# Gate and up projections with seven block products instead of eight, the middle channels in two rounds

## The chip, the cores and the metric

The kernel runs on one core of a Trainium2 chip. The metric is device time in microseconds (us) of one execution. TensorE is PE in the rows, VectorE DVE, ScalarE ACT, GpSimd POOL, and SyncE's queue, which issues the loads, SP.

## The reference

Two layers over 512 tokens of 1024 channels. Each layer has two feed-forward (FFN) parts around a mixer, and a per-layer embedding step at its end:

```python
def swiglu(x, w_gate, w_up, w_down):
    return (jax.nn.silu(x @ w_gate) * (x @ w_up)) @ w_down
...
for l in range(DEPTH):
    h = h + 0.5 * swiglu(rms_norm(h, ffn1_norm[l]), ffn1_w_gate[l], ffn1_w_up[l], ffn1_w_down[l])
    h = h + hybrid_mixer(rms_norm(h, mix_norm[l]), ...)
    h = h + 0.5 * swiglu(rms_norm(h, ffn2_norm[l]), ffn2_w_gate[l], ffn2_w_up[l], ffn2_w_down[l])
    gate = jax.nn.sigmoid(rms_norm(h, ple_norm[l]) @ ple_w_gate[l])
    h = h + gate * (p[l] @ ple_w_proj[l])
return rms_norm(h, final_norm)
```

The middle width of the FFN is 2816, that is 22 tiles of 128 channels; all data are float32.

## The kernel before

Channels lie on the partitions, the 512 tokens along the rows, so the residual stream `hT` is 8 tiles of 128x512. A float32 product is made of three products of float32r parts: each operand is split into a high and a low part (ACT copies the high part, DVE subtracts it from the value), and `mm3` issues high x high, high x low and low x high into one PSUM bank. Weights come in raw tiles `wr` of 512 KB (three buffers, loaded from SP) and are split into `wh` and `wl` (two buffers each).

PE takes its matmuls in the order in which they are written down. The other engines run their instructions in an order that the scheduler fixed when the program was built; each engine runs its own list strictly from front to back, so an instruction that waits holds all that stand behind it.

An FFN loops over the 22 middle tiles. For each it makes the gate product `pg` and the up product `pu`, 8 channel tiles x 3 matmuls of 128x512 each, and then `gated` works on the pair on DVE and ACT. The norm of the row isn't in the operand: the row factor `rb` is worked out beside the first products (`norm.sums` and `norm.rows`, which PE issues at the two places that `at` names) and multiplied in after the product. Then 8 output tiles `pd` of 22 x 3 matmuls follow, and after each one `residual` work on DVE and the split of the next part's operand (`Norm.add`).

There are four FFN parts: the first at the start of the program, the second behind the mixer's output projection (`pwo`), the third behind the embedding step of layer 0 (`ppg`), the fourth behind the second mixer.

## Time and profile before

| | |
|---|---|
| median of 3 runs | 2087.9 us (2087.01 to 2090.97) |
| profiled execution: span from first to last instruction | 2086.9 us (the profile gives no other time of this execution) |
| PE busy | 2042.6 us, 98% |
| DVE busy | 1108.8 us, 53% |
| ACT busy | 740.0 us, 35% |

The busy time of PE counts every matmul with its drain, and these overlap, so two neighbours are better compared by their starts. Whether PE really waits shows where its busy time in a window is below the window's length.

### The profile page before, as it was taken

What the parts mean: (1) busy time and instruction counts of PE and PEld (TensorE: products, weight loads), DVE (VectorE), ACT (ScalarE), POOL (GpSimd) and SP (SyncE); (2) the same over time, 40 slices, a digit from 0 to 9 for tenths busy, and PEclk for the clock granted to TensorE, in tenths of its full rate; (3) what the DMA queues carried; (4) which work ended last, traced back from release to release, by engine and by line L of the source; (5) the groups of instructions that cost most, each with busy time, mean ns of one, the idle gap of its engine ahead of it and who ended that gap; (6) DMA issues with size and microseconds to landing.
All of it is one profiled execution on the core that took longest, in us unless ns stands there. A gap on an engine that the chain in (4) does not pass through costs nothing.

```text
span 2086.9 us, 24214 instructions
## 1 busy us (share of the span) xinstructions
PE 2042.6 (98%) x9529; PEld 1666.5 (80%) x9529; DVE 1108.8 (53%) x1958; ACT 740.0 (35%) x1188; POOL 189.7 (9%) x166
## 2 busy tenths in 40 slices
PE   9999999998999999999999999999899999999997
PEld 6888888877778888888878888888676888888886
DVE  5444433779855444433754444337997644443346
ACT  4232223355643232223532222224475432222233
POOL 1000001052110000000100000000521100000002
PEclk9999999999999999999999999999999999999998
DMA  5323233311032223333323233333110332333331
GB/s 185 101 91 101 89 92 102 97 51 54 9 101 91 98 94 98 90 97 109 101 92 101 92 100 89 98 96 99 56 34 21 105 98 92 100 93 95 98 99 61
DMA packets 56290, 186.35 MB, mean 89 GB/s; under 512 B 6384, under 2 KB 9712, under 8 KB 55920
## 3 DMA queue, kind: packets, MB, share of 16 engines
q1 hardware_dynamic: 56176, 184.81, 28.3%
q8 instruction: 74, 1.21, 0.2%
q14 instruction: 40, 0.33, 0.0%
HBM read 182.69 MB, written 2.10 MB: 89 GB/s over the span
## 4 chain that ended last, share of the span: by engine, by line
PE 90%; DVE 6%; ACT 2%; issue 1%; DMA 1%; POOL 0%; SPq 0%; DVEq 0%; ACTq 0%; POOLq 0%
PE pd L141 8%; PE pd L143 8%; PE pu L143 8%; PE pd L142 8%; PE pu L142 8%; PE pu L141 8%; PE pg L143 8%; PE pg L142 7%; PE pg L141 7%; PE pp L141 2%; PE pp L143 2%; PE pp L142 2%; PE pwo L143 1%; PE pwo L141 1%; PE pwo L142 1%; PE ppg L142 1%
## 5 line engine op out<-in xcount | busy, mean ns | idle before, releaser
L117 ACT ACTIVATE wh<-wr 128x1024 fp32r<-128x1024 f32 (+1 forms) x346 | 356.9, 1031 | 1140.5 <-issue 741.7
L118 DVE TENSOR_TENSOR wl<-wr,wh 128x1024 fp32r<-128x1024 f32 (+1 forms) x334 | 397.8, 1191 | 355.8 <-ACT wh L117 355.6
L222 POOL TENSOR_TENSOR acc<-acc,sq 128x512 f32<-128x512 f32 (+1 forms) x55 | 80.8, 1469 | 1589.9 <-ACT sq L221 1589.3
L282 DVE TENSOR_TENSOR gs<-th,pu 128x512 f32<-128x512 f32 x88 | 60.4, 688 | 219.9 <-PE pu L143 219.9
L141 PE MATMUL pd<-h,wh 128*128 128x512 f32 x448 | 175.1, 391 | 0.0
L278 DVE TENSOR_TENSOR gs<-pg,rb 128x512 f32<-128x512 f32 x88 | 60.5, 691 | 215.6 <-PE pg L143 215.6
L143 PE MATMUL pd<-h,wl 128*128 128x512 f32 x448 | 174.8, 390 | 0.0
L142 PE MATMUL pd<-l,wh 128*128 128x512 f32 x448 | 174.3, 389 | 0.0
L141 PE MATMUL pg<-B,wh 128*128 128x512 f32 x352 | 138.0, 392 | 2.4 <-ACT wh L122 1.6
L143 PE MATMUL pu<-A,wl 128*128 128x512 f32 x352 | 138.7, 394 | 0.0
L143 PE MATMUL pg<-A,wl 128*128 128x512 f32 x352 | 138.7, 394 | 0.0
L143 PE MATMUL pg<-B,wl 128*128 128x512 f32 x352 | 138.4, 393 | 0.1
L142 PE MATMUL pg<-B,wh 128*128 128x512 f32 x352 | 137.8, 392 | 0.6 <-DVE B L212 0.6
L143 PE MATMUL pu<-B,wl 128*128 128x512 f32 x352 | 138.3, 393 | 0.0
L142 PE MATMUL pg<-A,wh 128*128 128x512 f32 x352 | 137.9, 392 | 0.0
L142 PE MATMUL pu<-A,wh 128*128 128x512 f32 x352 | 137.9, 392 | 0.0
L141 PE MATMUL pu<-B,wh 128*128 128x512 f32 x352 | 137.7, 391 | 0.0
L142 PE MATMUL pu<-B,wh 128*128 128x512 f32 x352 | 137.3, 390 | 0.0
L141 PE MATMUL pg<-A,wh 128*128 128x512 f32 x352 | 136.9, 389 | 0.0
L141 PE MATMUL pu<-A,wh 128*128 128x512 f32 x352 | 136.7, 388 | 0.0
L143 PE MATMUL pp<-B,wl 128*128 128x512 f32 x240 | 97.3, 405 | 6.6 <-DVE wl L118 6.6
L141 PE MATMUL pp<-B,wh 128*128 128x512 f32 x240 | 99.8, 416 | 0.0
(354 smaller groups left out, 3921.3 us busy)
## 6 DMA issues: line engine op xcount, KB each, us to landing
wr<-in_g_dram SPq DMA_DIRECT2D x87, 512.0 KB, 3.5
wr<-in_u_dram SPq DMA_DIRECT2D x87, 512.0 KB, 3.4
wr<-in_d_dram SPq DMA_DIRECT2D x64, 512.0 KB, 3.6
wr<-in_wi_dram SPq DMA_DIRECT2D x30, 512.0 KB, 3.4
wr<-in_d_dram SPq DMA_DIRECT2D x32, 384.0 KB, 3.1
wr<-in_pg_dram SPq DMA_DIRECT2D x16, 512.0 KB, 3.4
wr<-in_wo_dram SPq DMA_DIRECT2D x8, 512.0 KB, 3.5
wr<-in_wt_dram SPq DMA_DIRECT2D x8, 392.0 KB, 3.0
```

The costliest lines, as they stand in the source:

```text
L117: A.activation(out=hi, in_=raw, func=AF.Copy)
L118: (via or V).tensor_tensor(out=lo, in0=raw, in1=hi.bitcast(F32), op=ALU.subtract)
L141: T.matmul(out=out, lhsT=wh, rhs=xh, start=start, stop=False)
L142: T.matmul(out=out, lhsT=wh, rhs=xl, start=False, stop=False)
L143: T.matmul(out=out, lhsT=wl, rhs=xh, start=False, stop=stop)
L222: (V if k == KD - 1 else G).tensor_tensor(out=acc, in0=acc, in1=sq, op=ALU.add)
L278: V.tensor_tensor(out=gs, in0=pg, in1=norm.rb, op=ALU.mult)
L282: V.tensor_tensor(out=gs, in0=th, in1=pu, op=ALU.mult)
```

## The change

Two middle tiles, two halves of the 1024 channels (4 tiles each) and two halves of the tokens (256 each) make a product of 2x2 blocks. The change forms each such product by Strassen's scheme (in Winograd's form): 7 block products in place of 8. What was 2 x 8 x 3 matmuls of 512 columns becomes 7 x 4 x 3 matmuls of 256 columns. Such a block product for gate or for up is called a unit here; an FFN has 22 units (11 for the gate, 11 for up, in turn), the program 88.

- The operand side needs sums of blocks. `Norm.upper` and `Norm.lower` form them where the split of the operand stood, for each pair of channel tiles q and q + 4, and split each sum into two parts.
- The weight side needs four sums. `load` reads the 16 blocks' rows of a unit by three loads from SP (512, 512 and 256 KB) and one more 512 KB read that POOL issues and that adds into the second tile (`r2`, two buffers). `combine` forms the other sums with two DVE additions (L408 and L409 of the changed kernel) and splits the results. The names are A12 and A11 (split from the raw tile `r1`), S4 (split into `sh`, `sl`), S3 and S1 (from `r2`), A22 and S2 (from `r3`).
- `Unit.p` issues a block product (12 matmuls) and the copies and sums of its results: L463 and L464 after product 1, L467 after 7, L470 after 6, L472 after 4, L474 after 5. PE's order in a unit is 2, 1, 3, 7, then 5 of the unit before, then 6 and 4. In the first two units of an FFN it is 2 and 3 of both units (three of the four channel pairs, then the fourth), and then the rest.
- The middle channels go in two rounds (5 and 6 pairs of tiles); the down projection runs after each, with the residual added twice.
- The mixer's work buffers go from 20 to 14, and other tiles of it share the operand's places.

The rest of the diff renames tiles and moves loads. In the diff, `groups` are buffers for 8 blocks of split weights: five, used in turn.

```diff
-AT0 = (23, 31)
-AT1 = (15, 23)
-# columns of the constants
+AT0 = (12, 15)
+AT1 = (8, 12)
+NP = NF // 2
+ROUNDS = ((0, 5), (5, 11))
+NX = 4
...
+    class Combined:
+        def __init__(self):
+            self.t = {}
+        def at(self, part, n):
+            i = NT28 // 2 * part + n
+            if i not in self.t:
+                self.t[i] = place(i)
+            return self.t[i]
+        def __call__(self, part, name, q):
+            if name == "B11":
+                return self.at(part, 12 + q // 2)[:, H * (q % 2):H * (q % 2) + H]
+            n, c = {"B22": (0, 0), "B21": (0, H), "T3": (1, 0), "t2": (1, H), "t1": (2, 0), "T4": (2, H)}[name]
+            return self.at(part, 3 * q + n)[:, c:c + H]
...
+        def gained(self, k, cs, hi, lo):
             h, gk = hT[:, k, cs], self.gain[:, k:k + 1]
-            A.activation(out=self.xh[k][:, cs], in_=h, func=AF.Copy, scale=gk)
-            V.scalar_tensor_tensor(out=self.xl[k][:, cs], in0=h, scalar=gk, in1=self.xh[k][:, cs].bitcast(F32),
+            A.activation(out=hi, in_=h, func=AF.Copy, scale=gk)
+            V.scalar_tensor_tensor(out=lo, in0=h, scalar=gk, in1=hi.bitcast(F32), op0=ALU.mult, op1=ALU.subtract)
+        def split(self, k, t512, cs=ALL):
+            if not self.x:
+                self.gained(k, cs, self.xh[k][:, cs], self.xl[k][:, cs])
+            elif k < 4:
+                if cs.stop == S:
+                    self.upper(k, t512)
+            else:
+                self.lower(k - 4, cs)
+        def upper(self, q, t512):
+            x, h, gk = self.x, hT[:, q, :], self.gain[:, q:q + 1]
+            g, t14, t32 = t512("tg"), t512("t14"), t512("t32")
+            self.raw[q] = g, t14, t32
+            self.gained(q, HALVES[1], x(0, "B11", q), x(1, "B11", q))
+            A.activation(out=g[:, 0:H], in_=h[:, 0:H], func=AF.Copy, scale=gk)
+            V.scalar_tensor_tensor(out=t14[:, 0:H], in0=h[:, H:S], scalar=gk, in1=g[:, 0:H],
                                    op0=ALU.mult, op1=ALU.subtract)
+            split(t14[:, 0:H], x(0, "t1", q), x(1, "t1", q))
+        def lower(self, q, cs):
+            x, h = self.x, hT[:, q + 4, :]
+            gk, nk = self.gain[:, q + 4:q + 5], self.neg[:, q + 4:q + 5]
+            g, t14, t32 = self.raw[q]
+            self.gained(q + 4, cs, x.both(0, 0, q)[:, cs], x.both(1, 0, q)[:, cs])
+            if cs.start == 0:
+                V.scalar_tensor_tensor(out=t32[:, 0:H], in0=h[:, 0:H], scalar=gk, in1=g[:, 0:H],
+                                       op0=ALU.mult, op1=ALU.subtract)
+                V.scalar_tensor_tensor(out=t32[:, H:S], in0=h[:, 0:H], scalar=nk, in1=t14[:, 0:H],
+                                       op0=ALU.mult, op1=ALU.subtract)
+                split(t32, x.both(0, 1, q), x.both(1, 1, q))
+            if cs.stop == S:
+                V.scalar_tensor_tensor(out=t14[:, H:S], in0=h[:, H:S], scalar=nk, in1=t32[:, H:S],
+                                       op0=ALU.mult, op1=ALU.subtract)
+                split(t14[:, H:S], x(0, "T4", q), x(1, "T4", q))
...
+            groups = iter(range(1 << 20))
+            def group(k, n):
+                i = next(groups) % 5
+                if i < 2:
+                    return [whp.tile([128, k, n], F32R, tag=t, name=t) for t in ("wh", "wl")]
+                return [fp.tile([128, k, n], F32R, tag=t, name=t, bufs=3) for t in ("gh", "gl")]
+            def halfgroup():
+                return [fp.tile([128, 4, 128], F32R, tag=t, name=t, bufs=2) for t in ("sh", "sl")]
...
+            def load(j, m):
+                src = a[f"{m}{which}"][l, j]
+                r1 = loaded(src[:, 0:8], 8)
+                r2 = fp.tile([128, 8, 128], F32, tag="r2", name="r2", bufs=2)
+                nc.sync.dma_start(out=r2, in_=src[:, 4:12])
+                G.dma_start(out=r2.rearrange("p k n -> p (k n)"), in_=src[:, 8:16].rearrange("p k n -> p (k n)"),
+                            accum_op=ALU.add)
+                r3 = wrp.tile([128, 8, 128], F32, tag="wr", name="wr")
+                nc.sync.dma_start(out=r3[:, 0:4], in_=src[:, 12:16])
+                return r1, r2, r3
+            def combine(r1, r2, r3):
+                w = {}
+                def put(raw, *names):
+                    g = group(8, 128) if len(names) == 2 else halfgroup()
+                    split(raw, *g)
+                    for i, n in enumerate(names):
+                        w[n] = [t[:, 4 * i:4 * i + 4] for t in g]
+                put(r1, "A12", "A11")
+                V.tensor_tensor(out=r3[:, 4:8], in0=r2[:, 4:8], in1=r1[:, 4:8], op=ALU.add)
+                V.tensor_tensor(out=r1[:, 0:4], in0=r1[:, 0:4], in1=r3[:, 4:8], op=ALU.add)
+                put(r1[:, 0:4], "S4")
+                put(r2, "S3", "S1")
+                put(r3, "A22", "S2")
+                return w
+            def product(ps, w, wn, xn, start, stop, qs=range(4)):
+                (wh, wl), more = w[wn], not (start and stop)
+                for q in qs:
+                    xh, xl = x(0, xn, q), x(1, xn, q)
+                    for i, (l_, r_) in enumerate(((wh, xh), (wh, xl), (wl, xh))):
+                        T.matmul(out=ps, lhsT=l_[:, q, :], rhs=r_, start=start and q == 0 and i == 0,
+                                 stop=stop and q == 3 and i == 2, skip_group_check=more)
+            count = iter(range(1 << 20))
...
+            def gated(cg, cu, hi, lo):
+                rb = norm.rb.unsqueeze(1).to_broadcast([128, 2, S])
+                V.tensor_tensor(out=cg, in0=cg, in1=rb, op=ALU.mult)
+                th = ft.tile([128, 2, S], F32, tag="th", name="th")
+                for i in range(2):
+                    A.activation(out=th[:, i, :], in_=cg[:, i, :], func=AF.Tanh, scale=0.5 - i)
+                V.scalar_tensor_tensor(out=th, in0=th, scalar=1.0, in1=cg, op0=ALU.add, op1=ALU.mult)
+                V.tensor_tensor(out=th, in0=th, in1=cu, op=ALU.mult)
+                split(th, hi, lo)
...
+                def p(self, n, qs=range(4)):
+                    ps, wn, xn, start, stop = {
+                        1: (self.X[:, 1], "A11", "B11", True, False), 2: (self.X[:, 0], "A12", "B21", True, True),
+                        3: (self.Y[:, 0], "S4", "B22", True, True), 7: (self.Y[:, 1], "S3", "T3", True, False),
+                        6: (self.X[:, 1], "S2", "t2", False, False), 4: (self.Y[:, 1], "A22", "T4", False, True),
+                        5: (self.X[:, 1], "S1", "t1", False, True)}[n]
+                    product(ps, self.w, wn, xn, start, stop, qs)
+                    if 3 not in qs:
+                        return
+                    with tc.high_priority():
+                        if n == 1:
+                            self.c = ft.tile([128, 2, S], F32, tag="c" + self.m, name="c" + self.m)
+                            c11 = self.c[:, 0, H:S]
+                            A.activation(out=c11, in_=self.X[:, 0], func=AF.Copy)
+                            V.tensor_tensor(out=c11, in0=c11, in1=self.X[:, 1], op=ALU.add)
+                        if n == 7:
+                            self.ys = ft.tile([128, 2, H], F32, tag="ys", name="ys", bufs=2)
+                            A.activation(out=self.ys, in_=self.Y, func=AF.Copy)
+                        if n == 6:
+                            self.e = ft.tile([128, H], F32, tag="e", name="e", bufs=2)
+                            A.activation(out=self.e, in_=self.X[:, 1], func=AF.Copy)
+                        if n == 4:
+                            V.tensor_tensor(out=self.c[:, 1, H:S], in0=self.e, in1=self.Y[:, 1], op=ALU.add)
+                        if n == 5:
+                            V.tensor_tensor(out=self.c[:, :, 0:H], in0=self.X[:, 1].unsqueeze(1).to_broadcast([128, 2, H]),
+                                            in1=self.ys, op=ALU.add)
+                    taken()
...
+            src = a[f"d{which}"]
+            for r, (j0, j1) in enumerate(ROUNDS):
+                last = None
+                us = list(range(2 * j0, 2 * j1))
+                if r == 0:
+                    prepare(0)
+                    prepare(1)
+                    pair = [begin(u, r) for u in (0, 1)]
+                    for qs in (range(3), range(3, 4)):
+                        for unit in pair:
+                            unit.p(2, qs)
+                            unit.p(3, qs)
+                    gate, up = pair
+                    prepare(2)
+                    for n in (1, 7, 6, 4):
+                        gate.p(n)
+                    up.p(1)
+                    gate.p(5)
+                    for n in (7, 6, 4):
+                        up.p(n)
+                    last = up
+                    us = us[2:]
+                for u in us:
+                    unit = begin(u, r)
+                    if u + 1 < 2 * j1:
+                        prepare(u + 1)
+                    for n in (2, 1, 3, 7):
+                        unit.p(n)
+                    close(last)
+                    for n in (6, 4):
+                        unit.p(n)
+                    if unit.m == "g":
+                        gate = unit
+                    last = unit
+                close(last)
...
+                    pds = {}
+                    for d in range(KD):
+                        pds[d] = bank([128, S], "pd")
+                        down(pds[d], grouped(loaded(src[l, d][:, 0:8, :], 8), 8), range(8), range(8), True, False)
+                        if d == 0:
+                            continue
+                        for e in ((0, 1) if d == 1 else (d,)):
+                            end(e)
+                        if d == KD - 2:
+                            prepare(2 * j1)
...
-            dp = es.enter_context(tc.tile_pool(name="dp", bufs=20))
-            lp = es.enter_context(tc.tile_pool(name="lp", bufs=1))
-            ap_ = es.enter_context(tc.tile_pool(name="ap", bufs=1))
+            tp = es.enter_context(tc.tile_pool(name="tp", bufs=1, reuse_waits="tile"))
+            lp = es.enter_context(tc.tile_pool(name="lp", bufs=1, reuse_waits="tile"))
+            ap_ = es.enter_context(tc.tile_pool(name="ap", bufs=1, reuse_waits="tile"))
+            dp = es.enter_context(tc.tile_pool(name="dp", bufs=14, reuse_waits="tile"))
...
-            o[f"{n}{w}"] = i[f"ffn{w}_w_{s}"].reshape(L, KD, 128, NF, 128).transpose(0, 3, 2, 1, 4)
+            b = i[f"ffn{w}_w_{s}"].reshape(L, 2, 4, 128, NP, 2, 128)
+            b = np.stack([b[:, c, :, :, :, r] for r, c in ((0, 1), (0, 0), (1, 0), (1, 1))], 4)
+            o[f"{n}{w}"] = b.transpose(0, 3, 2, 4, 1, 5).reshape(L, NP, 128, 16, 128)
```

The order of instructions on DVE, in the steady part of an FFN. Before, the products of a pair of middle tiles are followed by the splits of the next weights (`wl`) and by the gating (L278, L281, L282, L123); `pg` and `pu` are the products:

```order
L278 TENSOR_TENSOR gs_5430<-pg_5374,rb_4969 128x512
L118 TENSOR_TENSOR wl_5441<-wr_5438,wh_5440 128x1024
L281 SCALAR_TENSOR_TENSOR th_5432<-th_5432,gs_5430 128x512
L282 TENSOR_TENSOR gs_5430<-th_5432,pu_5405 128x512
L118 TENSOR_TENSOR wl_5472<-wr_5469,wh_5471 128x1024
L123 TENSOR_TENSOR B15_4843<-gs_5430,B7_4835 128x512
```

After the change, in the second round of the first FFN. `cg_2672<-e_2736,qg_2622` (L472) is the last result of the unit that ends; it waits for the last product of that unit. `wr_2623` is the raw tile `r1` of the unit that PE takes next, `sh`/`sl` are the parts of its S4, `wr_2753`, `wr_2758` and `r2_2755` are the tiles of the unit after that, and X4/X5 are the parts of a gated result:

```order
L129 TENSOR_TENSOR gl_2631<-wr_2623,gh_2630 128x1024
L472 TENSOR_TENSOR cg_2672<-e_2736,qg_2622 128x256
L129 TENSOR_TENSOR X5_2715<-th_2717,X4_2714 128x1024
L409 TENSOR_TENSOR wr_2623<-wr_2623,wr_2628 128x512
L129 TENSOR_TENSOR gl_2761<-wr_2753,gh_2760 128x1024
L408 TENSOR_TENSOR wr_2758<-r2_2755,wr_2753 128x512
L129 TENSOR_TENSOR sl_2637<-wr_2623,sh_2636 128x512
```

The split of S4 for a unit stands behind L472 of the unit before and four more instructions.

The order on DVE where the second FFN starts. Before: `pwo_4778` is the last tile of the output projection, A14 and A15 are low parts of the operand, L222 is the last sum of squares:

```order
L997 TENSOR_TENSOR hT_75<-hT_75,pwo_4778 128x512
L118 TENSOR_TENSOR wl_4880<-wr_4877,wh_4879 128x1024
L212 SCALAR_TENSOR_TENSOR A15_4621<-hT_75,par_73,A7_4613 128x512
L222 TENSOR_TENSOR acc_4475<-acc_4475,sq_4806 128x512
L118 TENSOR_TENSOR wl_4938<-wr_4935,wh_4937 128x1024
L237 TENSOR_SCALAR nv_4913<-ssc_4908 128x4
```

After the change (the last additions to `hT` and its blocks stand just ahead): T25 is an operand part of the last channel pair, `wr_6163`, `wr_6168` and `r2_6165` belong to the first gate unit, `wr_6188`, `wr_6193` and `r2_6190` to the first up unit:

```order
L243 TENSOR_SCALAR neg_9857<-par_73 128x8
L129 TENSOR_TENSOR T25_6095<-t14_6088,T11_6094 128x256
L408 TENSOR_TENSOR wr_6168<-r2_6165,wr_6163 128x512
L409 TENSOR_TENSOR wr_6163<-wr_6163,wr_6168 128x512
L129 TENSOR_TENSOR wl_6181<-r2_6165,wh_6180 128x1024
L129 TENSOR_TENSOR gl_6185<-wr_6168,gh_6184 128x1024
L129 TENSOR_TENSOR gl_6196<-wr_6188,gh_6195 128x1024
L408 TENSOR_TENSOR wr_6193<-r2_6190,wr_6188 128x512
L129 TENSOR_TENSOR gl_6206<-r2_6190,gh_6205 128x1024
L129 TENSOR_TENSOR sl_6177<-wr_6163,sh_6176 128x512
L409 TENSOR_TENSOR wr_6188<-wr_6188,wr_6193 128x512
L129 TENSOR_TENSOR sl_6202<-wr_6188,sh_6201 128x512
```

The splits of S4 (`sl_6177`, `sl_6202`) now stand behind both units' sums and five splits.

And the steps of the norm, behind the last result (L472) of the first up unit of that FFN; `ny`, `nb`, `rh`, `rl` are tiles of 128x4, `sq_6383` is what `norm.rows` multiplies on PE, which PE issues right behind that unit's last product:

```order
L472 TENSOR_TENSOR cu_6358<-e_6426,qu_6216 128x256
L165 SCALAR_TENSOR_TENSOR ny_6368<-nb_6369,ny_6368 128x4
L129 TENSOR_TENSOR wl_6466<-r2_6450,wh_6465 128x1024
L166 SCALAR_TENSOR_TENSOR nb_6369<-ny_6368 128x4
L167 TENSOR_TENSOR nb_6369<-nb_6369,nv_6366 128x4
L168 SCALAR_TENSOR_TENSOR ny_6368<-nb_6369,ny_6368 128x4
L321 CAST rh_6380<-ny_6368 128x4
L325 TENSOR_TENSOR sq_6383<-cst_72,rh_6380 128x512
L323 TENSOR_TENSOR rl_6381<-ny_6368,rh_6380 128x4
L325 TENSOR_TENSOR sq_6383<-cst_72,rl_6381 128x512
```

The two `sq` tiles, the operands of `norm.rows`, now stand behind a result of the second unit and behind a weight split.

## Rows read from the trace of the kernel before

**Rows 1.** first line and section 1 of the page.
```profile
span 2086.9 us, 24214 instructions
PE 2042.6 (98%) x9529; PEld 1666.5 (80%) x9529; DVE 1108.8 (53%) x1958; ACT 740.0 (35%) x1188; POOL 189.7 (9%) x166
```

**Rows 2.** section 4 of the page, the chain that ended last, shares by engine.
```profile
PE 90%; DVE 6%; ACT 2%; issue 1%; DMA 1%; POOL 0%; SPq 0%; DVEq 0%; ACTq 0%; POOLq 0%
```

**Rows 3.** windows of two stages: sum, busy time (x instructions), clock, DMA, GB/s.
```profile
24.00:382.00 358.00, 357.90 (x1573) 293.77 (x1572) 159.16 (x221) 103.38 (x130) 10.91 (x8) 1.00 0.31 97
412.00:600.00 188.00, 176.03 (x1016) 139.02 (x1015) 148.87 (x416) 102.07 (x246) 51.61 (x49) 0.95 0.15 47
```

**Rows 4.** groups by form, one of twelve alike (four buffers sets, three lines).
```profile
L141 PE MATMUL pg<-A,wh 128*128 128x512 f32 x352 | 136.9, 389 | 0.0
```

**Rows 5.** timeline of PE, 45 matmuls of 512 columns, then 48 of 256.
```profile
1024.00 0.39 PE L141 MATMUL ppg<-A,wh 128*128 128x512 f32 x1
...
1034.07 0.39 PE L143 MATMUL ppg<-A,wl 128*128 128x512 f32 x1
1034.30 0.28 PE L141 MATMUL ppg<-A,wh 128*128 128x256 f32 x1
...
1039.83 0.28 PE L143 MATMUL ppg<-A,wl 128*128 128x256 f32 x1
```

**Rows 6.** groups by form, the weight loads of that stretch.
```profile
L142 PEld LDWEIGHTS ppg<-A,wh 128*128 128x128 f32 x152 | 28.6, 188 | 4.0
```

**Rows 7.** timeline of DVE, neighbours in three stretches.
```profile
704.79 1.23 DVE L118 TENSOR_TENSOR wl<-wr,wh 128x1024 fp32r<-128x1024 f32 x1 [0.22 <-ACT wh L117]
705.93 0.68 DVE L281 SCALAR_TENSOR_TENSOR th<-th,gs 128x512 f32<-128x512 f32 x1
...
893.30 0.69 DVE L312 SCALAR_TENSOR_TENSOR dt<-pd,rb 128x512 f32<-128x512 f32 x1 [1.99 <-PE pd L143]
894.03 0.69 DVE L313 TENSOR_TENSOR hT<-hT,dt 128x512 f32<-128x512 f32 x1
894.64 1.22 DVE L118 TENSOR_TENSOR wl<-wr,wh 128x1024 fp32r<-128x1024 f32 x1
...
1038.37 0.41 DVE L1030 TENSOR_TENSOR gs<-ppg,rb 128x256 f32<-128x256 f32 x1
1038.70 0.68 DVE L1033 TENSOR_TENSOR hT<-hT,gs 128x512 f32<-128x512 f32 x1
```

**Rows 8.** timeline of ACT, one high part of a weight tile.
```profile
709.19 1.06 ACT L117 ACTIVATE wh<-wr 128x1024 fp32r<-128x1024 f32 x1 [3.91 <-issue]
```

**Rows 9.** timelines of PE and DVE, a last matmul and its reader.
```profile
703.45 0.39 PE L143 MATMUL pg<-A,wl 128*128 128x512 f32 x1
...
703.88 0.69 DVE L278 TENSOR_TENSOR gs<-pg,rb 128x512 f32<-128x512 f32 x1 [2.75 <-PE pg L143]
```

**Rows 10.** timelines of PE and ACT at the program's start.
```profile
14.81 0.39 PE L141 MATMUL pu<-B,wh 128*128 128x512 f32 x1
...
4.62 1.28 ACT L211 ACT_TABLE_LOAD   x1 [4.62 <-DMA hT<-in_x_dram]
5.92 0.72 ACT L211 ACTIVATE B<-hT,par 128x512 fp32r<-128x512 f32 x1
```

**Rows 11.** timeline of PE, start of the third feed-forward part.
```profile
1045.73 0.51 PE L141 MATMUL pg<-B,wh 128*128 128x512 f32 x1 [0.81 <-ACT B L211]
```

**Rows 12.** timeline of DVE, small steps of the norm.
```profile
633.07 0.16 DVE L150 TENSOR_SCALAR ni<-nv 128x4 int32<-128x4 int32 x1
633.27 0.17 DVE L152 TENSOR_SCALAR ny<-ni 128x4 int32<-128x4 int32 x1
```

**Rows 13.** section 6 of the page, one kind of weight load.
```profile
wr<-in_g_dram SPq DMA_DIRECT2D x87, 512.0 KB, 3.5
```

**Rows 14.** timelines of DVE and POOL, the same stretch.
```profile
600.27 3.49 DVE L212 SCALAR_TENSOR_TENSOR A<-hT,par,A 128x512 fp32r<-128x512 f32 x2
...
600.21 3.01 POOL L222 TENSOR_TENSOR acc<-acc,sq 128x512 f32<-128x512 f32 x2 [0.94 <-ACT sq L221]
```

290 lines of the change are left out of this document (174 added, 116 removed).

## The prediction

> **What bounds the kernel now.** I read the page's first line and shares, then the chain that ended last, then two windows, then PE's timeline. PE is busy for 2042.6 of 2086.9 us [rows 1] and holds 90% of the chain [rows 2]. In the first FFN it is busy without a gap at the full granted clock, while DVE is busy for 159 of 358 us; near the mixer's end PE loses 12 of 188 us [rows 3]. So inside an FFN only the number of matmul columns counts, as long as DVE and ACT keep up, and whatever the change adds there lies at first in DVE's free 55%. The gate and up products are twelve groups of 352 matmuls [rows 4]: 4224 of 512 columns. The profiled span of 2086.9 us stands 1.0 us below the median of 2087.9; the sum is made on the span and the 1.0 added at its end. A measurement of this kernel tells 0.2% (4 us) from no change.
>
> **What is saved.** The timeline has both widths behind each other. From 1024.00 to 1034.07 are 44 steps of 512 columns, 0.2289 us each; from 1034.30 to 1039.83 are 47 of 256, 0.1177 us each [rows 5]. The half-width matmul costs 51.4% of the whole. 4224 x 0.22886 = 966.7 us become 88 x 7 x 12 = 7392 matmuls x 0.11766 = 869.7 us: **-97.0 us**, 1.10 per unit (10.99 to 9.88). The down projections keep their matmuls; the second addition of the residual lies on DVE beside them.
>
> The Trainium skill speaks against narrow matmuls: the page "TensorE: Matmul & The Clock Gate", Part 3, section "The mechanism", says that a weight load is overlapped with a running matmul only when the row group differs. By that each of these would pay its load. The rows don't agree: the loads take 188 ns [rows 6], each matmul has its own, and the pitch of 256 columns is still 0.118 us. By the rule the sum would stand some 1390 us higher; I keep it as the last rival.
>
> **DVE in the steady part.** Pitches of neighbours: 1024 elements 1.14 us, 512 elements 0.61, a dependent 512 0.73, 256 elements 0.33 [rows 7]. A unit has three splits of 1024, one of 512 and two additions of 512: 3 x 1.14 + 3 x 0.61 = 5.25. Its results are two of 256 and one of 512: 1.27. Half of a gating with four of 1024: 2.28. Together 8.80 of 9.88 us, 89%. ACT's 1024 takes 1.06 at most [rows 8]; with some five and a half such per unit it is behind. DVE isn't the bound by throughput, but it has 1.1 us of slack, and its list is fixed. So the order decides.
>
> **S4 late: +37 us.** The second piece of the order shows L472, which waits for the unit's last product, and behind it the split of X, L409, a split of 1024, L408, and only then the split of S4 of the unit that PE has just begun. A reader starts 0.04 us after the end of the last matmul [rows 9]; a matmul of 256 columns lasts 0.28 [rows 5], so 0.20 after its pitch. Then S4 is there 0.20 + 0.33 + 1.14 + 0.61 + 1.14 + 0.61 + 0.61 = 4.64 us after the unit's end. PE needs it for product 3's second or third matmul, after 26 matmuls: 3.06 us. That is 1.6 us of PE wait. I counted this pattern (S4 behind the L472 of the unit before and four others) in DVE's order in 23 of the 88 units, 5 in the first FFN and 6 in each other: 23 x 1.6 = 37. In the rest S4 stands ahead of L472, and nothing is added.
>
> **The norm's rows: +15 us.** `norm.rows` now stands right behind the first up unit (the first FFN: 36 matmuls later), and DVE's last steps for it stand behind that unit's L472. In FFNs 2 to 4: 0.20 + 0.33 + a split of 1.14 + two `sq` of 0.61 + six small steps of 0.20 [rows 12] = 4.1 us of wait each. In the first: 0.20 + 0.33 + 2 x 1.14 + 3 x 0.61 + 12 x 0.20 = 7.04, less 36 x 0.118 = 4.24, so 2.8. Together 15. Before, this stood behind whole products, and rows 3 show no gap.
>
> **The program's start: +19.5 us.** Before, PE starts the second product (the 25th matmul) at 14.81 us [rows 10]; 24 matmuls are 5.5, so 9.3 us have been lost. ACT has `hT` at 4.62, loads its table for 1.28 and copies [rows 10]; DVE can begin at about 6.4. Until the up unit's S4 is split its list has 28 instructions of 256, 15 of 512 and 5 of 1024: 28 x 0.33 + 15 x 0.61 + 5 x 1.14 = 24.1, and some 12 dependent steps at 0.12 more, so 32.0 us. PE waits there with 27 of the first pair's 168 matmuls done, since the fourth channel pair of products 2 and 3 comes ahead of everything else; the other 141 take 16.6, to 48.6. Without loss 168 take 19.8, so 28.8 us are lost instead of 9.3. A restart after a pause may run at the lower pitch, as in the first matmuls of the third FFN at 0.51 a piece [rows 11]: nothing to 1.5 us at each of the four starts; I take nothing.
>
> **Three other starts: +31 us.** Behind the last addition to `hT`, DVE has (third piece of the order and the blocks ahead of it) 4 instructions of 256, 8 of 512 and 4 of 1024 until S4 of the gate unit: 1.3 + 4.9 + 4.6 = 10.8, with 0.2 for the reader and 0.8 for ACT's copies between 11.8. PE has 9 matmuls for that time, 1.1 us; the wait is 10.7. Before, the third FFN's start shows 0.81 us idle [rows 11]; 1.0 is set off for it, and nothing at the others: 3 x 10.7 - 1.0 = 31. There DVE and POOL also slow each other: two L212 take 3.49 us together beside POOL's two `acc` additions in place of 2 x 0.73 [rows 14]; the six `acc` additions of the change stand ahead of POOL's accumulating read. This may add 2 us a start; in the range.
>
> The Trainium skill's page "SBUF — State Buffer", section "Who interferes with whom", says that DVE with two SBUF inputs contends with GpSimd's reads; the rows just named agree.
>
> **Prices that no row has.** The accumulating read by POOL: a plain load of 512 KB takes 3.5 us [rows 13], the bound below. Of two units' 19.8 us, some 6.7 lie, by the order and the durations above, between L408 and the end of the split that frees `r2`; 3.5 go to the first load, and 9.5 are left for the second read. Up to there it is hidden; beyond, each us costs half a us per unit (two buffers), 44 us in all. I take the value nearest to the row, hidden. The mixer's 14 buffers in place of 20: its windows have 12 us of PE idle [rows 3], so from -5 to +10 each, twice; I take 0.
>
> The Trainium skill prices a transfer that POOL issues in "DMA: Bandwidth & Descriptors", section "Anatomy of one DMA — SWDGE (gpsimd) path", at about 2 us and the bytes by 436 GB/s, an estimate of 3.2 us here. No run so far shows one; it leaves the sum as it is.
>
> **Sum.** 2086.9 - 97.0 + 37 + 15 + 19.5 + 31 = 2092.4, and 1.0 to the median: **2093 us**.
>
> **Rivals and chances.**
> A, the sum (0.52): 2070 to 2120, by the mixer (-10 to +20), the clock (0 to +6), the contention at starts (0 to +8) and the DVE waits a quarter off (+-13). Of this 0.12 is faster, 0.10 same, 0.30 slower.
> B, faster (0.34): the waits in the FFNs don't appear, because DVE's work between L472 and S4 is shorter than its neighbours' pitches elsewhere say, or because after one wait DVE has caught up and the next is smaller. For it: DVE's average of 89% leaves slack. Against: the fixed order, in which L472 can't start early. It decides where the chain of 4.64 us falls below 3.06. Without these two terms 2093 - 52 = 2041; with half of them, 2067; with a cheaper start, 2033.
> C, clearly slower (0.13): the accumulating read takes over 9.5 us, L408 waits, and with it all of DVE behind it. For it: it reads and writes SBUF, and it is queued on an engine with other work; against: 3.5 us for the plain one, and 97 GB/s of load [rows 3] are far from what 512 KB in 3.5 us (150 GB/s) show. At 10.5 us 2137, at 12 us 2203.
> D (0.01): weight loads that don't hide at 256 columns, 0.306 in place of 0.118 us: 7392 x 0.188 = +1390 against the hidden case, near 3480.
> That the change doesn't do what it says is excluded: the order has 7392 matmuls of 256 columns.
> The range, 2032 to 2135, holds A and nearly all of B and leaves C and D out. Faster 0.12 + 0.34 = 0.46, same 0.10, slower 0.30 + 0.13 + 0.01 = 0.44. A's own range is 2070 to 2120.
>
> **What would show it.** Pitch of L420's matmuls at 0.118. PE idle of 10 to 11 us at the start of FFNs 2 to 4, and about 20 more at the program's, with L129 of `sl` on DVE as what ends it. In steady units, waits of about 1.6 us before product 3, some 23 of them, and about 4 us before `norm.rows`. DVE busy for about 89% of those windows. POOL-issued reads that land within 9.5 us. It is wrong if DVE's pitches differ, if L408 waits for a DMA in steady units, or if the mixer's windows change by more than 10 us.

## The result, and the profile after

The changed kernel takes 2225.2 us (median of 4 runs, 2224.3 to 2228.0) against 2089.4 for the kernel before: a ratio of 1.065 (95% interval 1.0635 to 1.0665), 136 us slower. That is beyond the range that was forecast. The first line and the shares of the page, which answer to [rows 1]:

```profile
span 2224.0 us, 32435 instructions
PE 2012.1 (90%) x12697; PEld 1781.5 (80%) x12697; DVE 1574.1 (71%) x2578; ACT 1007.1 (45%) x1648; POOL 261.0 (12%) x254
```

PE has 30 us less of busy time and 137 us more of span: it now waits for a tenth of it. The windows show where. Each FFN now has two stretches of gate and up products, one for each round. The columns are those of [rows 3]: length, then busy time of PE, PEld, DVE, ACT and POOL, then the granted clock:

```profile
9.98:161.60 151.62, 113.05 (x849) 108.53 (x850) 114.84 (x157) 75.01 (x116) 21.75 (x18) 0.86 0.58 156
216.90:348.60 131.70, 123.31 (x1009) 120.97 (x1008) 99.95 (x123) 68.22 (x97) 7.78 (x9) 0.99 0.54 146
659.10:797.60 138.50, 111.18 (x851) 107.41 (x851) 98.22 (x137) 65.41 (x95) 11.84 (x13) 0.90 0.58 152
...
sum 1096.92, PE 937.13 PEld 911.80 DVE 813.48 ACT 545.46 POOL 88.15; mean PE 117.14 PEld 113.97 DVE 101.68 ACT 68.18 POOL 11.02
```

The same stretches of the kernel before, four windows from the first to the last gate or up product of each FFN, have this sum:

```profile
sum 976.20, PE 974.57 PEld 798.01 DVE 465.73 ACT 293.06 POOL 10.85; mean PE 243.64 PEld 199.50 DVE 116.43 ACT 73.27 POOL 2.71
```

976.2 us have become 1096.9. The 4224 old matmuls by their pitch were 966.7, so 9.5 us were lost there before; the 7392 new ones are 869.7, so **227 us are lost now**. The saving of 97 us is there (some 6800 of the new matmuls start within 0.13 us of the one before, 0.117 on average), and more than twice as much is lost beside it. The first rounds are the worst, with 165 of the 227 us and a clock of 0.86 to 0.92, and DVE, at 74% of the stretches, isn't full in any of them. The other 16 us of the 137 lie outside: 2.7 in the two mixers with their output projections, 9.7 in the two embedding steps with the end of the program, 2.8 until the first product, the rest at the handovers between rounds.

The waits of PE in all of the program, longest first in total. Each line names who waited, behind the arrow the releaser (what ended the wait), then us in total, times, longest:

```profile
PE qg L420 <- ACT sh L128: 49.3, 5, 13.8
PE qg L420 <- DVE sl L129: 26.7, 16, 5.7
PE pg L420 <- DVE cg L464: 22.6, 13, 4.1
PE prow L334 <- DVE sq L325: 19.6, 6, 5.5
PE qu L420 <- DVE sl L129: 14.3, 15, 1.4
PE pu L420 <- DVE cu L464: 11.3, 8, 2.3
...
PE qg L420 <- DVE gl L129: 6.5, 4, 2.9
```

`sh` and `sl` are S4's parts, and `prow` the norm's rows: these three were forecast. The waits for `cg` and `cu` (L464) and for `gl` were not. DVE's own waits at L408, ahead of them in its list, point to the cause:

```profile
DVE wr L408 <- issue: 63.4, 12, 7.7
...
DVE wr L408 <- DMA wr<-in_g_dram: 29.9, 17, 7.1
...
DVE wr L408 <- DMA r<-in_g_dram: 8.7, 3, 6.9
...
DVE wr L408 <- DMA wr<-in_u_dram: 6.7, 8, 2.7
```

DVE stands still at L408 for 108.7 us in 40 places. "issue" means that the profile sees no releaser; the timelines of one such place show it to be POOL's read (DVE first, then the queue of SP, POOL and PE):

```profile
100.49 1.22 DVE L129 TENSOR_TENSOR wl<-r,wh 128x1024 fp32r<-128x1024 f32 x1
...
106.42 0.68 DVE L129 TENSOR_TENSOR sl<-wr,sh 128x512 fp32r<-128x512 f32 x1
112.72 0.69 DVE L408 TENSOR_TENSOR wr<-r,wr 128x512 f32<-128x512 f32 x1 [5.62 <-issue]
...
119.93 0.41 DVE L464 TENSOR_TENSOR cg<-cg,pg 128x256 f32<-128x256 f32 x1
...
101.73 0.33 SPq L391 DMA_DIRECT2D r<-in_u_dram  x1
...
105.95 0.86 POOL L392 DMA_DIRECT2D r<-in_u_dram  x1 [14.59 <-DMA r<-in_u_dram]
...
120.40 0.50 PE L420 MATMUL pg<-T,wh 128*128 128x256 f32 x2 [2.34 <-DVE cg L464]
...
121.68 0.63 PE L420 MATMUL pg<-T,wh 128*128 128x256 f32 x2
...
122.33 0.63 PE L420 MATMUL qg<-T,wh 128*128 128x256 f32 x2
```

The split that frees `r2` ends at 101.7 us. SP issues the next load at once, POOL can issue its read at 105.95, after the load has landed, and L408 gets its data at 112.72, 11.0 us after the split. DVE's list had come to L408 at 107.1. Everything behind it on DVE is 5.6 us late, L464 among it, and PE's product 6, which may only write its bank when L464 has read it, waits 2.34 us at 120.40. Behind that wait eight matmuls keep their pace, and then, from 121.47 to 124.86, sixteen start 0.21 us apart (121.68 to 122.33: three in 0.65): the granted clock is 0.50 there, the 1.2 GHz level.

At all 12 places with the releaser "issue" (63.4 us, 3.5 to 7.7 each) it is the same: on DVE's timeline L408 stood 5.4 to 5.8 us behind the end of the split that frees its buffer, while load and read took 9.3 to 13.1 us. In the units where L408 didn't wait, its place was 10.5 us or more behind that split. Three more places are like the 12: at the second gate unit of FFNs 2 to 4 L408 stood 6.6 us behind the split, the read landed 11.5 to 13.4 us behind it, and DVE waited for 5.7 to 7.1 us (at two of them a raw tile landed 0.7 us later still). The queue's own figures, us from issue to landing:

```profile
r<-in_g_dram SPq DMA_DIRECT2D x44, 512.0 KB, 3.8
...
r<-in_g_dram POOLq DMA_DIRECT2D x44, 512.0 KB, 6.2
...
r<-in_u_dram POOLq DMA_DIRECT2D x44, 512.0 KB, 5.6
```

The read lands 5.6 to 6.2 us after its issue, the load of the same size into the same tile after 3.8 to 4.2 (the loads of raw tiles for gate and up now after 4.7 to 5.1; before 3.5, [rows 13]).

### The profile page after: what moved, and what is told of

Read it like the earlier page. It is cut to its first block, busy times and chain, and to the rows that moved or that the text cites. A ratio compares the mean times of both kernels' runs of the same rounds, so it can differ in the third digit from the quotient of the medians.

```text
span 2224.0 us, 32435 instructions
## 1 busy us (share of the span) xinstructions
PE 2012.1 (90%) x12697; PEld 1781.5 (80%) x12697; DVE 1574.1 (71%) x2578; ACT 1007.1 (45%) x1648; POOL 261.0 (12%) x254
## 5 line engine op out<-in xcount | busy, mean ns | idle before, releaser
L129 DVE TENSOR_TENSOR gl<-wr,gh 128x1024 fp32r<-128x1024 f32 x148 | 181.5, 1228 | 76.9 <-ACT gh L128 76.0
L129 DVE TENSOR_TENSOR wl<-wr,wh 128x1024 fp32r<-128x1024 f32 x108 | 132.0, 1222 | 132.3 <-ACT wh L128 132.2
L128 ACT ACTIVATE gh<-wr 128x1024 fp32r<-128x1024 f32 x148 | 155.7, 1055 | 153.6 <-PE pd L148 90.6
L420 PE MATMUL pg<-T,gh 128*128 128x256 f32 x896 | 163.2, 281 | 10.4 <-DVE cg L464 10.3
L420 PE MATMUL pu<-T,gh 128*128 128x256 f32 x832 | 154.7, 284 | 5.4 <-DVE cu L464 4.6
L420 PEld LDWEIGHTS pg<-T,gh 128*128 128x128 f32 x896 | 137.1, 188 | 12.0 <-DVE cg L464 11.6
L408 DVE TENSOR_TENSOR wr<-r,wr 128x512 f32<-128x512 f32 x88 | 60.6, 688 | 108.8 <-issue 63.4
L123 ACT ACTIVATE wh<-wr 128x1024 fp32r<-128x1024 f32 (+2 forms) x76 | 77.0, 1014 | 130.8 <-PE pp L148 43.3
L420 PEld LDWEIGHTS pu<-T,gh 128*128 128x128 f32 x832 | 129.6, 192 | 7.2 <-DVE cu L464 5.8
L420 PE MATMUL pg<-T,gl 128*128 128x256 f32 x448 | 126.1, 281 | 1.2 <-DVE gl L129 0.5
L420 PE MATMUL pg<-T,wh 128*128 128x256 f32 x512 | 104.3, 301 | 19.8 <-DVE cg L464 12.3
L420 PE MATMUL pu<-T,gl 128*128 128x256 f32 x416 | 118.4, 285 | 0.9 <-DVE gl L129 0.2
L148 PE MATMUL pd<-X,wh 128*128 128x512 f32 x288 | 112.6, 391 | 0.0
L147 PE MATMUL pd<-X,wh 128*128 128x512 f32 x288 | 112.6, 391 | 0.0
```

The lines of the kernel that those rows point to most:

```text
L123: A.activation(out=hi, in_=raw, func=AF.Copy)
L128: A.activation(out=hi, in_=x, func=AF.Copy)
L129: V.tensor_tensor(out=lo, in0=x, in1=hi.bitcast(F32), op=ALU.subtract)
L147: T.matmul(out=out, lhsT=wh, rhs=xh, start=start, stop=False)
L148: T.matmul(out=out, lhsT=wh, rhs=xl, start=False, stop=False)
L408: V.tensor_tensor(out=r3[:, 4:8], in0=r2[:, 4:8], in1=r1[:, 4:8], op=ALU.add)
```

## The experiments

Two theories were set against each other first. **R**: the accumulating read comes late, L408 blocks DVE's list, and banks and weight parts come late for PE. **O**: DVE's list is too full or badly ordered anyway, and L408 only marks the place. Times are medians; the changed kernel is 2225.2, and the ratios are to the kernel before, run beside each (2087.9 to 2089.6). For each kernel the scheduler makes DVE's list anew.

**no_accumulate**

```diff
-                G.dma_start(out=r2.rearrange("p k n -> p (k n)"), in_=src[:, 8:16].rearrange("p k n -> p (k n)"),
-                            accum_op=ALU.add)
```

> The accumulating read by POOL is left out, so S3 and S1 hold only their first summand (that part of the computation is missing); everything else stays, and the scheduler makes its lists anew. Theory R (the read is late, L408 waits for it at the head of DVE's list, 108 us in all, and PE then finds its banks not freed and its weight parts not split): the waits of L408 fall to under 10 us, the waits of PE for L464, L467 and for gl (about 53 us, and about 19 us of matmuls at the lower clock behind them) go, and the time falls by 55 to 75 us to 2150 to 2170 us. Rival O (DVE's list is overfull and badly ordered anyway, L408 only marks the place): under 20 us of gain, 2205 us or more, and DVE's idle time turns up at other lines.

Measured 2169.5 us, 1.038 (1.0361 to 1.0402): 55.7 us won. What is left of DVE's waits at L408, all for raw tiles:

```profile
DVE wr L408 <- DMA wr<-in_g_dram: 14.4, 11, 3.2
...
DVE wr L408 <- DMA wr<-in_u_dram: 4.8, 6, 2.5
```

19 us in place of 108.7, where under 10 was expected. PE's waits for L464 and L467 together fall from 37 to 13 us, those for `gl` from 8 to 2, and the sum of the eight stretches falls by 61 us, to 1035.7. R holds, at the lower end of its gain. DVE has as much to do as in the changed kernel (806.6 against 813.5 us in the stretches), and 2533 of its 2578 instructions stand in the same sequence, so O, which had under 20 us, doesn't. But 12 of the 61 us lie in the program's first stretch, and these aren't L408's alone: POOL's six additions of squares run at 30.8 to 40.5 us there instead of 21.7 to 34.3, no longer beside DVE's first weight splits (first_squares_on_vector shows what that costs), and DVE's list for that start is in another order.

**accumulate_an_eighth**

```diff
-                G.dma_start(out=r2.rearrange("p k n -> p (k n)"), in_=src[:, 8:16].rearrange("p k n -> p (k n)"),
+                G.dma_start(out=r2[:, 7], in_=src[:, 15],
                             accum_op=ALU.add)
```

> POOL's read adds into one of the eight rows of the tile (64 KB in place of 512; the other seven rows lack their second summand), so the chain load, POOL's issue, second landing stays, and DVE's list stays nearly as it was. Theory R with the transfer as the cost: it lands about 3 us sooner than the 5.6 to 6.2 us after its issue, half of L408's waits go, gain 25 to 45 us (2180 to 2200). If the fixed part of a second read behind a first is the cost, it lands hardly sooner and the gain is under 15 us. Rival O: under 10 us.

Measured 2172.8 us, 1.040 (1.0377 to 1.0421): 52.5 us won, more than either side expected. The read now lands in less than half of the time:

```profile
r<-in_g_dram POOLq DMA_DIRECT2D x44, 64.0 KB, 2.7
```

Some 3 us less per read bring nearly all that leaving it out brings. At the 12 places DVE now stands for 0.7 to 3.6 us, 19 us together in place of 63.4, and PE's waits for L464 and L467 fall from 37 to 12 us.

**three_r2_buffers**

```diff
-                r2 = fp.tile([128, 8, 128], F32, tag="r2", name="r2", bufs=2)
+                r2 = fp.tile([128, 8, 128], F32, tag="r2", name="r2", bufs=3)
...
-                            self.e = ft.tile([128, H], F32, tag="e", name="e", bufs=2)
+                            self.e = ft.tile([128, H], F32, tag="e", name="e", bufs=1)
```

> Three buffers for r2 in place of two (and one for e in place of two, to make room), nothing else. Theory R with the buffer as the cause (the first load can't begin before the split of two units before has freed the tile, and only then comes the read): the loads start a unit earlier, L408's waits for the read fall to below 20 us of the 72 us that are not for raw tiles, gain 40 to 60 us (2165 to 2185). If the raw tiles wr, three buffers for two per unit, hold the loads back just as much, L408 waits for wr instead and the gain is under 15 us. Rival O: none.

Measured 2179.6 us, 1.044 (1.0414 to 1.0465): 45.7 us won. No wait of L408 with releaser "issue" is left; those for raw tiles (33 us) and for `r2` at two starts (2) are:

```profile
DVE wr L408 <- DMA wr<-in_g_dram: 25.9, 13, 6.5
```

The read itself is as slow as in the changed kernel (5.6 and 6.3 us), but it no longer stops DVE once it starts a unit earlier. So the wait was the buffer's: the chain of load and read could only begin when the split of two units before was done. The run also answers a rival, the traffic of the read: leaving it out takes the second round of the first FFN from 146 to 115 GB/s and from 131.7 to 126.5 us; the third buffer leaves 143 GB/s and brings 126.8 us.

**seven_before_three**

```diff
...
-                        if n == 7:
+                        if n == (3 if late else 7):
...
-                    for n in (2, 1, 3, 7):
-                        unit.p(n)
+                    for n in (2, 1, 7, 3):
+                        unit.p(n, late=True)
```

> In the steady units PE takes product 7 ahead of product 3, so that the split of S4 has 12 matmuls (1.41 us) more; the copy of both goes behind product 3. Theory S (S4's split is late by 1.2 to 1.5 us in each of some 30 units because it stands behind L472 of the unit before): these waits, 38 us and some 8 us of lower clock, nearly go, and 30 to 45 us are won (2180 to 2195). Rival: the wait moves to the split of S3 for product 7, or to the banks that DVE frees late, and the gain is under 15 us.

Measured 2172.1 us, 1.039 (1.0365 to 1.0417): 53.1 us won. (Product 3 opens the bank anew here, so that product 7's part is missing from the results; the number of matmuls is the same.) The place that S4 was forecast to be late at, in the changed kernel:

```profile
124.86 0.39 PE L420 MATMUL pu<-T,wh 128*128 128x256 f32 x2
...
129.68 0.38 PE L420 MATMUL qu<-T,sl 128*128 128x256 f32 x1 [1.18 <-DVE sl L129]
...
125.13 0.42 DVE L472 TENSOR_TENSOR cg<-e,qg 128x256 f32<-128x256 f32 x1 [1.79 <-PE qg L420]
...
128.95 0.68 DVE L129 TENSOR_TENSOR sl<-wr,sh 128x512 fp32r<-128x512 f32 x1
```

The unit before ends at 124.86. L472 follows, the split of X, L409, a split of 1024, L408, and S4's split ends at 129.6, 4.8 us behind the unit's end: 4.64 were worked out. PE had come to it at about 127.9 and stood 1.8 us, 1.18 of them in one piece. With product 7 first the waits of `qg` and `qu` for `sl` fall from 31 to 11 times, those for both parts of S4 from 93 to 64 us. The gain is 8 us above the top of the theory's, for PE's waits for L464 fall too, from 34 to 18 us.

**seven_first_three_buffers** joins the last two edits; whichever of 3 and 7 comes first opens the bank:

```diff
-                        3: (self.Y[:, 0], "S4", "B22", True, True), ...
+                        3: (self.Y[:, 0], "S4", "B22", 7 not in self.done, True), ...
```

> Three buffers for r2 (and one for e) together with product 7 ahead of product 3 (whichever comes first clears the bank's accumulation). Alone they gave 46 and 53 us. If they mend two different things (the late read that stops DVE at L408, and S4 behind L472), they add up to 85 to 100 us: 2125 to 2140. If product 7 first won its time because it absorbed the same DVE delay, 60 to 75 us: 2150 to 2165.

Measured 2157.5 us, 1.032 (1.0291 to 1.0358): 67.8 us won, where the two alone sum to 98.8. The sum of the eight stretches is 1018.0 us, 78.9 less than in the changed kernel, where the two alone won 47.1 and 53.5 there; the difference is lost in the mixers, 12.6 us longer at a granted clock of 0.93 (see rows_later). So the whole time falls to the second theory, while the stretches lie between the two: 22 us of the two gains by the stretches, 31 by the whole time, were the same delay of DVE. How product 7 first shortens it isn't shown: no more matmuls stand between products 1 and 6 than before, but DVE's list was made anew, with 2471 of 2578 instructions in the same sequence.

**start_with_one**

```diff
-                        1: (self.X[:, 1], "A11", "B11", True, False), ...
+                        1: (self.X[:, 1], "A11", "B11", 2 not in self.done, False), ...
...
                         for unit in pair:
                             unit.p(2, qs)
-                            unit.p(3, qs)
+                            unit.p(1, qs)
...
-                    for n in (1, 7, 6, 4):
+                    for n in (3, 7, 6, 4):
                         gate.p(n)
-                    up.p(1)
+                    up.p(3)
```

> In the first two units of an FFN PE takes products 2 and 1 early (three channel pairs of both units, then the fourth), and product 3 with its S4 comes behind them. Before the first matmul that needs S4, PE then has 48 matmuls instead of 9, 4.6 us more work. Theory D (S4's two additions and splits are what PE waits for, 10.6 to 13.8 and then 1.8 to 5.7 us): each start is shorter by about 4 to 4.6 us, 15 to 20 us together (about 2207). Rival (products 2 and 1 need the splits of both raw tiles and come as late in DVE's list, the whole list is what lasts): under 7 us, the 21 matmuls fewer behind the last split at 0.118 us, 2.5 us a start at most.

Measured 2207.7 us, 1.056 (1.0536 to 1.0583): 17.6 us won, in sum as theory D had it (15.7 in the stretches). PE's two long waits at each of the four starts fall together by 4.4, 3.5, 3.0 and 3.2 us, less than D's 4 to 4.6 in three of them, and more than the rival's 2.5 at most. The start of the second FFN in the changed kernel (DVE's last addition to `hT`, S4's split; then PE):

```profile
661.40 0.68 DVE L1281 TENSOR_TENSOR hT<-hT,pwo 128x512 f32<-128x512 f32 x1
...
673.14 0.68 DVE L129 TENSOR_TENSOR sl<-wr,sh 128x512 fp32r<-128x512 f32 x1
...
671.27 0.80 PE L420 MATMUL qg<-T,sh 128*128 128x256 f32 x2 [10.86 <-ACT sh L128]
...
673.88 0.58 PE L420 MATMUL qg<-T,sl 128*128 128x256 f32 x1 [1.82 <-DVE sl L129]
```

From the last addition to the low part of S4 are 11.7 us (662.1 to 673.8; 11.8 were worked out). PE stands for 10.9 and 1.8 us, 12.7 where 10.7 were worked out: its last matmul for `pwo` is done at 659.15, and DVE comes to the addition only 2.2 us later.

**rows_later**

```diff
-AT1 = (8, 12)
+AT1 = (8, 15)
```

> The norm's row products are issued three block products (36 matmuls, 4.24 us) later in FFNs 2 to 4; the sums stay. Theory N (DVE's last steps for them stand behind L472 of the unit just done and are 3.7 us late in each, and the matmuls behind run at the lower clock for 1.1 to 1.9 us): the three waits go, and 13 to 17 us are won (about 2209). Rival: the row factor comes later too, the gating on DVE with it, and the banks are freed later by as much; gain under 5 us.

Measured 2238.4 us, 1.071 (1.0685 to 1.0726): 13.1 us slower, which neither expected. The rows' wait became shorter in two of the three FFNs, but a new one stands behind it (PE, second FFN):

```profile
709.15 0.50 PE L334 MATMUL prow<-sq,ones_r 128*128 128x512 f32 x1 [3.53 <-DVE sq L325]
...
718.53 0.80 PE L420 MATMUL pg<-T,gh 128*128 128x256 f32 x2 [4.52 <-DVE cg L464]
```

The sum of the eight stretches is 1098.7 us, as good as unchanged: there the rival holds. The loss lies in the mixers, which the edit doesn't touch, in the profiled run. The window of the first here, and in the changed kernel:

```profile
412.30:574.30 162.00, 152.01 (x735) 124.91 (x733) 134.01 (x330) 77.68 (x155) 43.86 (x41) 0.92 0.18 59
```

```profile
414.40:569.50 155.10, 144.50 (x737) 118.59 (x735) 134.91 (x330) 77.02 (x154) 44.74 (x41) 0.97 0.19 62
```

It is 6.9 us longer at a granted clock of 0.92 in place of 0.97; the second mixer is 5.5 us longer at 0.92 in place of 0.96. DVE is as busy. Why the clock falls lower there isn't settled; single mixers of 155 to 163 us occur among the other kernels too. So a difference under some 10 us between these kernels is read from the stretches, not from the whole time.

**four_together** joins seven_first_three_buffers, start_with_one (product 1 doesn't open the bank where 2 came first) and rows_later.

> Those two edits together with the row products three block products later and the start with products 2 and 1. If all four are separate losses: 85 to 100 and 13 to 17 and 15 to 20 off 2225, 2088 to 2112, level with the kernel before or up to 1% above it. If later row products only delay the gating, or the start is bound by DVE's whole list: 2115 to 2135.

Measured 2133.7 us, 1.022 (1.0202 to 1.0233): 91.5 us won (99.4 in the stretches), the second theory's 2115 to 2135. Its largest waits in the steady part, one of 4.5 to 6.8 us in each FFN, show what later rows do (DVE, then PE, second FFN):

```profile
680.35 1.23 DVE L435 TENSOR_TENSOR cg<-cg,rb 128x1024 f32<-128x1024 f32 x1 [0.26 <-ACT rb L336]
...
683.15 1.22 DVE L439 SCALAR_TENSOR_TENSOR th<-th,cg 128x1024 f32<-128x1024 f32 x1
...
686.55 0.41 DVE L466 TENSOR_TENSOR cg<-cg,pg 128x256 f32<-128x256 f32 x1
...
687.02 0.80 PE L420 MATMUL pg<-T,gh 128*128 128x256 f32 x2 [4.52 <-DVE cg L466]
```

The gating L435 waits for the row factor `rb`; until L439 and L440 are through, the one buffer `cg` is taken; L466 (L464 in the changed kernel) can't write the next gate unit's `cg`, and PE's product 6 waits 4.52 us for it. The wait for the rows was moved, not removed.

**four_sums_earlier**

```diff
-AT1 = (8, 15)
+AT1 = (4, 12)
```

> As four_together, but in FFNs 2 to 4 the norm's sums are issued four block products earlier and the row products three earlier. Theory G (the gating of the first pair waits for the row factor, holds the one buffer cg, L466 of the next gate unit waits for it and PE's product 6 for L466: 4.5 to 6.8 us in each FFN, with up to 2.4 us of lower clock behind): both the waits at the row products and those at L466 fall to under 2 us each in these three FFNs, 15 to 22 us are won, about 2115. Rival (DVE's twelve small steps and two products of the identity now stand ahead of the splits for the start, and the start lasts longer by 3 to 4 us in each): gain under 8 us.

Measured 2120.8 us, 1.0155 (1.0138 to 1.0172): 12.9 us won, between the two; in the profiles the stretches are 17.4 us shorter (997.5 to 980.1), the waits for `cg` fall from 20.9 to 8.4 us. G holds. This is the fastest of the kernels that compute everything, and 33 us slower than the kernel before (2087.9 beside it).

**first_squares_on_vector**

```diff
...
-                (V if k == KD - 1 else G).tensor_tensor(out=acc, in0=acc, in1=sq, op=ALU.add)
+                (e or (V if k == KD - 1 else G)).tensor_tensor(out=acc, in0=acc, in1=sq, op=ALU.add)
...
         for k in range(KD):
-            norm.square(k, t512)
+            norm.square(k, t512, e=V)
```

> At the program's start alone, the six additions of squares that POOL makes go to DVE. Theory C (DVE and POOL slow each other there: between 23.9 and 34.2 us of the changed kernel DVE's instructions take up to twice their time, so that the low part of the first S4 comes at 38.2 us where 32 was forecast): although DVE has 3 to 4 us more work, the low part of the first S4 comes 3 to 5 us sooner, and the first stretch of gate and up products lasts 146 to 148 us in place of 151.6. Rival (the slow stretch is something else, the loads' traffic): it comes as late or later, the stretch stays at 151 to 154 us.

Measured 2218.4 us, 1.063 (1.0605 to 1.0661): 6.9 us won. By the whole time that isn't clear of the mixers' variation (the profiled run is 1.7 us longer than that of the changed kernel), so the start decides. The program's start in the changed kernel (DVE, POOL, PE), and then here (DVE, PE):

```profile
28.55 2.42 DVE L409 TENSOR_TENSOR wr<-wr 128x512 f32<-128x512 f32 x1
30.89 2.28 DVE L129 TENSOR_TENSOR gl<-wr,gh 128x1024 fp32r<-128x1024 f32 x1
...
28.84 5.44 POOL L298 TENSOR_TENSOR acc<-acc,sq 128x512 f32<-128x512 f32 x3
...
31.68 0.80 PE L420 MATMUL qg<-T,sh 128*128 128x256 f32 x2 [13.82 <-ACT sh L128]
38.17 0.58 PE L420 MATMUL qg<-T,sl 128*128 128x256 f32 x1 [5.70 <-DVE sl L129]
```

```profile
25.69 0.68 DVE L409 TENSOR_TENSOR wr<-wr 128x512 f32<-128x512 f32 x1
26.29 1.21 DVE L129 TENSOR_TENSOR gl<-wr,gh 128x1024 fp32r<-128x1024 f32 x1
...
31.44 0.58 PE L420 MATMUL qg<-T,sl 128*128 128x256 f32 x1 [2.32 <-DVE sl L129]
```

Beside POOL's additions L409 takes 2.42 us and a split of 1024 2.28; without them 0.68 and 1.21. PE gets S4's low part at 31.44 instead of 38.17, though two of the additions stand ahead of it on DVE. The first stretch falls from 151.6 to 144.3 us, more than C had. C holds, and the rival doesn't: from 22 to 34 us the DMAs move 189 GB/s here, 131 in the changed kernel. [rows 14] look the same. The Trainium skill, page "SBUF — State Buffer", section "Who interferes with whom", says that a DVE instruction with two SBUF inputs contends with a GpSimd instruction that reads SBUF; L409 in the two timelines agrees (2.42 and 0.68 us).

**four_sums_earlier_no_accumulate** is four_sums_earlier without the accumulating read.

> The kernel before it without POOL's accumulating read (S3 and S1 lack their second summand). If the third buffer has taken all of the read off DVE's list, there is nothing left to win: within 8 us of that kernel. If the read still costs (its write and read of SBUF, its place in POOL's list), 15 us or more are won. Were this kernel under 2089, the read would be all that stands between the change and a gain.

Measured 2093.8 us, 1.0025 (1.0006 to 1.0043): another 26.9 us, so the third buffer hadn't taken all of the read's cost away. The stretches are 24 us shorter (955.9), 18.5 of them in the four first rounds, and 9.6 of these in the program's first. L408 didn't wait for the read there; with the read POOL's additions of squares run at 21.9 to 35.1 us, beside DVE's weight splits (L409 takes 2.20 us), without it at 32.6 to 44.6 (0.68). What the read still costs in the other stretches isn't shown. Even so this kernel isn't faster than the kernel before.

**no_weight_sums**

```diff
-                G.dma_start(out=r2.rearrange("p k n -> p (k n)"), in_=src[:, 8:16].rearrange("p k n -> p (k n)"),
-                            accum_op=ALU.add)
...
-                nc.sync.dma_start(out=r3[:, 0:4], in_=src[:, 12:16])
+                nc.sync.dma_start(out=r3, in_=src[:, 8:16])
...
-                V.tensor_tensor(out=r3[:, 4:8], in0=r2[:, 4:8], in1=r1[:, 4:8], op=ALU.add)
-                V.tensor_tensor(out=r1[:, 0:4], in0=r1[:, 0:4], in1=r3[:, 4:8], op=ALU.add)
```

> The changed kernel without any sum of weight blocks: no accumulating read, no L408 and L409 (the seven products are formed from the loaded blocks as they are, one load is 512 KB in place of 256), so that DVE has 1.2 us less per unit and S4's split hangs on no other instruction. The operand's sums and the order on PE stay. If the 7392 half-width matmuls are worth what the pitch says (97 us less than before), and the losses stem from the weight sums and their order, the read's 56 us, S4's 45 to 50 and part of each start go: 2090 to 2115. If the seven products lose their time elsewhere (operand, results, banks, lower clock), it stays above 2150.

Measured 2088.4 us, 1.0005 (0.9994 to 1.0017): 136.8 us won, a little more than the first theory had. The weight sums, with their read, their place in DVE's list and their work there, are what separates the changed kernel from the kernel before; this run doesn't part the three. The sum of the stretches:

```profile
sum 957.10, PE 905.18 PEld 891.74 DVE 714.54 ACT 552.41 POOL 13.74; mean PE 113.15 PEld 111.47 DVE 89.32 ACT 69.05 POOL 1.72
```

19 us less than before where 97 are saved. Of the 87 us that are still lost, 82 lie in the first rounds, where PE waits at the starts, for the norm's rows and for L464, with the lower clock behind. The mixers (9.5 us longer than before in the profiled run) and the rest outside the stretches take the 19 us back. With free weight sums, and the rest as written, the change would be level.

## Why the prediction was wrong

The time, 2225, lies above the range (2032 to 2135). The mechanism was the one of rival C, which had 0.13 and prices of 2137 at 10.5 us and 2203 at 12, but not by its condition, a read of over 9.5 us: the read took 5.6 to 6.2. Of the prediction's own signs of being wrong one came true, L408 waiting for a DMA in steady units.

**The step that failed** is the cover of the accumulating read, "9.5 are left for the second read". It was worked out from the mean: two units' 19.8 us less 6.7. Load and read together took mostly 9 to 13 us, so by the mean cover of 13.1 the read would have been hidden in nearly all units, and in most it was. But DVE's list isn't a mean. At 12 places L408 stands 5 to 6 us of work behind the split that frees its buffer, DVE's other work waits there for 63 us (109 with the waits for raw tiles and at the starts), and PE feels it at banks and weight parts that the prediction had put at nothing: 46 us of waits for L464, L467 and `gl`, besides the lower clock behind them. Taking the read out won 55.7 us (12 of the 61 in the stretches by the program's start, see there), shortening it 52.5, a third buffer 45.7. The place could have been read from the order: the distance on DVE between the split of one `r2` and the next L408 on the same buffer, unit by unit, as was done for S4.

**The other step that failed** is the restart, "nothing to 1.5 us at each of the four starts; I take nothing". Matmuls that didn't wait but started later than 0.1177 us behind their neighbour add up to 44.5 us, some 30 of them where the granted clock is 0.50. The starts cost 1.8 to 2.9 us each that way, more than the term's upper end, and waits in the steady part, which the term left out, are followed by the 1.2 GHz level too: eight times 1.5 us, behind waits of 1.9 to 4.1 us.

**What was right, and by how much** (from the brackets of the changed kernel's PE timeline):

- The saving: -97 us by the pitch, which stands.
- S4 late: +37 forecast. The waits for `sh` and `sl` are 93.3 us, of which 59.8 are the four starts; 33.5 remain.
- The norm's rows: +15 forecast, 13.9 measured (2.65, and three of 3.73 or 3.74). Not foreseen: the gating waits for the same factor, so that later rows win nothing (rows_later).
- Three other starts: 32 us of wait forecast, 40.2 measured. The chain behind the last addition lasted as worked out in the second FFN, but DVE came to that addition 2.2 us after PE's last matmul in the second and fourth (12.7 and 12.4, where 10.7 were worked out); the third FFN's is 15.2.
- The program's start: 28.8 us lost forecast, 39.1 measured (36 matmuls done at 43.34), 7 of the difference through POOL's additions, which the text had put in the range at 2 us a start.
- The mixers with 14 buffers: nothing forecast, 2.7 us measured. The embedding steps with the program's end, which the sum doesn't name: 9.7.
- DVE at 89% of the steady part: 73 to 76% in the second rounds, with 8.3 us a unit in place of 8.80, and units of 11.0 to 11.4 us in place of 9.88.

The Trainium skill's price for a transfer that POOL issues ("DMA: Bandwidth & Descriptors", section "Anatomy of one DMA — SWDGE (gpsimd) path"), an estimate of 3.2 us for 512 KB, is half of the 5.6 to 6.2 us that this accumulating read took; for the 64 KB of accumulate_an_eighth the estimate by it is 2.15 us, and 2.6 to 2.7 were measured. The measurement decides; no run here issued a plain read of that size from POOL, so how much of the difference is the accumulation isn't shown.

What stays open: why the mixers' granted clock is lower in some kernels, what the read still costs with three buffers, and how much of the 227 us belongs to the operand's sums alone, which no kernel left out.
